# Decay tables of a gated-DeltaNet / S5 trunk: built from a float32 product on TensorE instead of from broadcast loads, and stored once per chunk from ScalarE's queue

## The chip, the cores and the metric

The kernel runs on one core of one Trainium2 chip. The metric is the device time of one execution in microseconds (us), the median of several runs. "PE" is TensorE's matmul stream, "PEld" its weight loads, "DVE" VectorE, "ACT" ScalarE, "POOL" GpSimd, "SP" SyncE, which here does nothing but issue DMAs. "PEclk" is the share of full TensorE clock that was granted.

## What is computed

One layer over a prompt of 4096 frames and over 32 frames of a running stream, with D_MODEL 1024. Half of the width goes through a gated delta rule with 4 heads of 128, the other half through an S5 state space. The delta rule is evaluated in chunks; this kernel takes chunks of 128 frames, so 32 of them for the prompt and one for the short stream, 33 in all. The part of the reference that the change touches is the decay between two frames of a chunk, which scales both the triangular system and the attention inside the chunk:

```python
    gc = jnp.cumsum(g, axis=-1)
    diff = gc[..., :, None] - gc[..., None, :]
    decay = jnp.where(incl, jnp.exp(jnp.where(incl, diff, 0.0)), 0.0)
    kb = k * beta[..., None]
    lower = jnp.where(strict, jnp.einsum('nbhid,nbhjd->nbhij', kb, k) * decay, 0.0) + eye
    attn = jnp.where(incl, jnp.einsum('nbhid,nbhjd->nbhij', q, k) * decay, 0.0)
```

## The kernel before

The program has three parts, recorded one after the other, and a tile scheduler orders each engine's instructions at build time from that recording and from priorities.

**Part A** normalises x, writes it to DRAM as two float16 halves (`h_d`), projects the S5 input and the gate logits, runs the S5 scan in four blocks of 1024 frames, and works out the two gate projections `z` (`zproj`, lines 505 to 526). One unit of `zproj` takes 128 frames: two transposing DMAs from `h_d` into `hz0` and `hz1` (line 519, issued by SP, two buffers each), 24 matmuls of 128x128x512 (line 492), a tanh on ACT (line 524), a multiply on DVE (line 525), and a store to `z_d` issued by POOL (line 526). There are 33 units for the gate of the delta rule and then, after the weights in `wz` have been replaced, 33 for the gate of S5 (`zs`). They have a low priority and fill gaps.

At the end of part A come the **tables**. `gates` has left the running decay sums `gc` in DRAM (`gc_d`, one row of 128 per head and chunk), half the beta values in `be_d`, and minus the sums by partition in `ngC` (in the buffer `gcC`). For each chunk, `tables` (line 985) loads the row of sums of its four heads onto all 128 partitions (line 990, a broadcast from DRAM into `tdm`), and the betas likewise (line 992, into `tbr`); POOL sets everything under the diagonal to -1e30 (line 993); ACT takes four exponentials with the negative sums as bias (line 995); POOL multiplies betas and decay (line 997); SP stores both tables to `dm_d` (lines 998 and 999). `tdm` and `tbr` have three buffers each.

**Part B** runs the chunks. Four chunk generators (`par` 0 to 3) interleave with a stream of dense work (q/k/v projections, S5 output). Its pools take over the memory of part A, so the first chunk's loads wait for the last unit of `zproj`. A chunk (line 1436 on) loads the chunk's decay sums' exponentials into `gr` by a broadcast (line 1480) and its two tables into `br` and `dm` (lines 1482 and 1483). POOL multiplies `kn` by `ed` (line 1519) and `qT` by `gr` (line 1522); DVE multiplies the key product by `br` (line 1532, giving the triangular system `at` for `inverse`) and the query product by `dm` (line 1543). Line 1456 is the helper that splits a float32 tile into two float16 halves, and line 48 the helper through which most matmuls go.

**Part C** is the output projection of what part B left over.

Of the kernel before, what the change touches and what calls it, by code (L numbers as in the profile page):

```python
# [6 lines left out]
F32 = mybir.dt.float32  # L7
# [4 lines left out]
ALU = mybir.AluOpType  # L12
# [5 lines left out]
H = 4  # L18
# [17 lines left out]
class Drive:  # L36
# [3 lines left out]
    def __init__(self, nc):  # L40
        self.nc, self.t, self.streams = nc, 0.0, []
# [38 lines left out]
class Trunk:  # L80
    def __init__(self, ctx, tc, io, T):
        self.ctx, self.tc, self.nc, self.io, self.T = ctx, tc, tc.nc, io, T
        self.NB = T // 512
        self.NC = T // 128
        nc = self.nc
        self.pe = Drive(nc)
        self.ugs = []
        self.ws, self.un, self.uz, self.marks = {}, {}, {}, []
        self.cst = ctx.enter_context(tc.tile_pool(name="cst", bufs=1))
        self.sm = ctx.enter_context(tc.tile_pool(name="sm", bufs=2))  # L90
        self.dram = ctx.enter_context(tc.tile_pool(name="dram", bufs=1, space=DRAM))
        c = self.cst
        self.ident = c.tile([128, 128], F32, name="ident")
        self.ones_pool = ExitStack()
        self.ones = self.pool(self.ones_pool, "a_one").tile([128, 128], F32, name="ones")
        nc.gpsimd.memset(self.ones, 1.0)
        nc.gpsimd.affine_select(out=self.ident, in_=self.ones, pattern=[[1, 128]], compare_op=ALU.is_equal,
                                fill=0.0, base=0, channel_multiplier=-1)
        self.mhalf = c.tile([128, 4], F32, name="mhalf")
        nc.gpsimd.memset(self.mhalf, -0.5)  # L100
        self.ident16 = c.tile([128, 128], F16, name="ident16")
        nc.vector.tensor_copy(self.ident16, self.ident)
        self.h_d = [self.dram.tile([2, 1024, 1024], F16, name=f"h_d{b}") for b in range(T // 1024)]
        self.hs_d = self.dram.tile([2, TS, 1024], F16, name="hs_d")
        self.us_d = self.dram.tile([512, 8, TS // 8], F32, name="us_d")
        self.ab_d = self.dram.tile([64, T // 1024, 128], F32, name="ab_d")
        self.abs_d = self.dram.tile([8, 128], F32, name="abs_d")
        self.gy_d = [self.dram.tile([4, 128, 1024], F32, name=f"gy_d{b}") for b in range(T // 1024)]
        self.gys_d = self.dram.tile([4, 128, TS], F32, name="gys_d")
        self.z_d = [self.dram.tile([1024, 512], F32, name=f"z_d{b}") for b in range(T // 1024)]  # L110
        self.zs_d = self.dram.tile([TS, 512], F32, name="zs_d")
        self.z5_d = [self.dram.tile([1024, 512], F32, name=f"z5_d{b}") for b in range(T // 1024)]
        self.z5s_d = self.dram.tile([TS, 512], F32, name="z5s_d")
        self.mx_d = [self.dram.tile([2, 256, 512], F16, name=f"mx_d{b}") for b in range(T // 256)]
        self.mxs_d = self.dram.tile([2, TS, 512], F16, name="mxs_d")
        self.m5_d = [self.dram.tile([2, 1024, 512], F16, name=f"m5_d{b}") for b in range(T // 1024)]
        self.m5s_d = self.dram.tile([2, TS, 512], F16, name="m5s_d")
        self.gc_d = {"p": self.dram.tile([H, self.NC, 128], F32, name="gc_d"), "s": self.dram.tile([H, 1, 128], F32, name="gcs_d")}
        self.be_d = {"p": self.dram.tile([H, self.NC, 128], F32, name="be_d"), "s": self.dram.tile([H, 1, 128], F32, name="bes_d")}
        self.eg_d = {"p": self.dram.tile([H, self.NC, 128], F32, name="eg_d"), "s": self.dram.tile([H, 1, 128], F32, name="egs_d")}  # L120
        self.dm_d = [self.dram.tile([2, 128, H, 128], F32, name=f"dm_d{c}") for c in range(self.NC + 1)]
        self.kp_d = self.dram.tile([16, 2, G, 240], F16, name="kp_d")


# [109 lines left out]
    def phase_a(self):  # L234
        nc, io = self.nc, self.io
# [53 lines left out]
        for blk in range(NK):  # L289
# [7 lines left out]
            if blk == NK - 3:  # L297
# [9 lines left out]
                f, ws = self.wfirst("zs", self.room_pr())  # L307
# [11 lines left out]
        bld = ExitStack()  # L319
# [13 lines left out]
        self.e_gy = cst.tile([128, 2], F32, name="e_gy")  # L333
        self.pow2(ma, self.e_gy[:, 0:1], self.e_gy[:, 1:2])
        self.right.close()
        tbl = self.pool(bld, "b_tbl")
        order = list(range(self.NC))
        order.insert(2 * SP, self.NC)
        with self.tc.high_priority(offset=-250):
            for ci in order:  # L340
                self.tables(tbl, ci)
        self.phase_b1()
        bld.close()
        left.close()
# [637 lines left out]
        self.ngC = self.gcC  # L982
        v.tensor_single_scalar(self.ngC, self.gcC, -1.0, op=ALU.mult)

    def tables(self, pool, ci):

        nc = self.nc
        key, cd = ("p", ci) if ci < self.NC else ("s", 0)
        dm = pool.tile([128, H, 128], F32, name="tdm", bufs=3)
        nc.sync.dma_start(dm, self.gc_d[key][:, cd].partition_broadcast(128))  # L990
        br = pool.tile([128, H, 128], F32, name="tbr", bufs=3)
        nc.sync.dma_start(br, self.be_d[key][:, cd].partition_broadcast(128))
        nc.gpsimd.affine_select(out=dm, in_=dm, pattern=[[0, H], [1, 128]], compare_op=ALU.is_ge, fill=-1e30, base=0, channel_multiplier=-1)  # L993
        for h in range(H):
            self.last_exp = nc.scalar.activation(dm[:, h], dm[:, h], AF.Exp, bias=self.ngC[:, h, ci:ci + 1])  # L995
            self.after(self.last_exp, self.last_gelu)
        nc.gpsimd.tensor_tensor(br, br, dm, op=ALU.mult)
        nc.sync.dma_start(self.dm_d[ci][0], dm)
        nc.sync.dma_start(self.dm_d[ci][1], br)

    def scales(self):

# [421 lines left out]
    def chunk(self, ci, c, b, key, par):  # L1424

        nc, ck, pc, pe = self.nc, self.ck, self.pc, self.pe
        pf = self.pf
        v, gp, act = nc.vector, nc.gpsimd, nc.scalar
# [5 lines left out]
        def t4(nm, dt=F32, n=128):  # L1434
            return ck.tile([128, H, n], dt, name=f"{nm}{par}")
# [4 lines left out]
        def col(t):  # L1440
            return t[:, :, ci:ci + 1].to_broadcast([128, H, 128])
# [4 lines left out]
        def tmp():  # L1446
            return ck.tile([128, H, 128], F32, name="tp", bufs=2)

        def halves(t):
            return t.rearrange("p h c -> p (h c)").bitcast(F16).rearrange("p (x h c) -> p x h c", x=2, h=H)  # L1450

        def pair(t, src, eng=gp):

            t, n = halves(t), src.shape[-1]
            act.copy(t[:, 0, :, :n], src)
            eng.tensor_tensor(t[:, 1, :, :n], src, t[:, 0, :, :n], op=ALU.subtract)
            return t
# [21 lines left out]
        cd = ci if key == "p" else 0  # L1479
        nc.sync.dma_start(gr, self.eg_d[key][:, cd].partition_broadcast(128))  # L1480
        br, dm = t4("br"), t4("dm")
        nc.sync.dma_start(br, self.dm_d[ci][1])
        nc.sync.dma_start(dm, self.dm_d[ci][0])

        yield lambda: not self.busy
        while self.busy:
# [31 lines left out]
        t = tmp()  # L1518
        gp.tensor_tensor(t, kn, col(self.ed), op=ALU.mult)
        kd = pair(kn, t)  # L1520
        t = tmp()
        gp.tensor_tensor(t[:, :, :m], qT[:, :, ts], gr[:, :, :m], op=ALU.mult)
        if m < 128:
# [18 lines left out]
        t = tmp()  # L1542
# [338 lines left out]
```

## Time and profile before

| | us |
|---|---|
| median of 3 runs (lowest, highest) | 2684.92 (2680.22, 2686.32) |
| the profiled execution | 2683.79 |
| its span | 2682.1 |
| PE busy | 2106.2 (79%) |
| DVE busy | 1588.1 (59%) |
| ACT busy | 1203.1 (45%) |
| POOL busy | 973.6 (36%) |
| SP's DMA queue, share of 16 DMA engines | 44.9% |

The busy shares are means over parts that differ: part A ends at some 1180 us of the span, part B at some 2300 us. The page's row of 40 slices shows PE at 3 to 4 tenths from slice 10 to slice 15, where it is at 7 to 9 tenths before and after; that stretch is where the tables are made.

### The profile page before, as it was taken

Reading aid. Unit: us, or ns where it says so; the run is one execution under the profiler, and the core shown is the slowest. Engines: PE = TensorE matmul, PEld = TensorE weight load, DVE = VectorE, ACT = ScalarE, POOL = GpSimd, SP = SyncE. Lnnn points to the kernel's source line nnn. Section 1 sums busy time; section 2 is a strip of 40 time slices with the busy share of each in tenths; the row PEclk is TensorE's granted clock in tenths of the full one; section 3 lists DMA queues with packets and bytes.
Section 4 is the critical chain, followed back from the end, with each engine's and each line's share of the span. In section 5 each row is a group of like instructions: output and inputs, shape, how many; then the busy total and the mean of one; then the engine's idle time right before and its main releaser. Section 6 shows DMA issues by size and latency. Waiting matters only on the chain.

```text
span 2682.1 us, 47343 instructions
## 1 busy us (share of the span) xinstructions
PE 2106.2 (79%) x17712; PEld 1481.7 (55%) x17712; DVE 1588.1 (59%) x3855; ACT 1203.1 (45%) x3400; POOL 973.6 (36%) x1080
## 2 busy tenths in 40 slices
PE   3887788768374445888988788788988986899998
PEld 3544666645142112546767677677777874454443
DVE  3796665777151000336978789877878897533222
ACT  5355455324352111225666566666656766321111
POOL 1354354434122122123554455445544554310000
PEclk9988899879687777989999999899989997899999
DMA  4489577366876778353223332222313235256552
GB/s 150 147 200 220 117 161 161 59 71 129 149 179 132 138 146 162 79 106 77 69 65 81 72 79 75 72 70 76 77 59 78 78 99 135 61 150 176 148 149 82
DMA packets 498847, 303.94 MB, mean 113 GB/s; under 512 B 346676, under 2 KB 447256, under 8 KB 498104
## 3 DMA queue, kind: packets, MB, share of 16 engines
q1 hardware_dynamic: 488392, 266.85, 44.9%
q0 software_dynamic: 10224, 34.06, 4.2%
q8 instruction: 138, 2.26, 0.4%
q14 instruction: 93, 0.76, 0.1%
HBM read 128.22 MB, written 94.88 MB: 83 GB/s over the span
## 4 chain that ended last, share of the span: by engine, by line
PE 29%; DVE 15%; DMA 9%; issue 5%; ACT 5%; POOL 3%; SPq 2%; POOLq 0%; DVEq 0%; ACTq 0%
PE pp L48 15%; PE po L48 7%; DVE acc L1332 3%; PE pz L492 3%; PE bk L48 3%; DMA hz<-h_d 3%; DMA m_d<-gh 3%; ACT jk L1495 1%; DMA tdm<-gc_d 1%; PE bk L52 1%; DVE kn L1596 1%; SPq L519 1%; DVE qT L1338 1%; DVE ubd L1653 1%; DMA tbr<-be_d 1%
## 5 line engine op out<-in xcount | busy, mean ns | idle before, releaser
L492 PE MATMUL pz<-wz,hz 128*128 128x512 f16 (+1 forms) x1464 | 390.3, 411 | 207.3 <-DMA hz<-h_d 178.5
L492 PEld LDWEIGHTS <-hz 128*128 128x128 f16 (+1 forms) x1464 | 148.1, 104 | 417.9 <-DMA hz<-h_d 211.7
L1332 DVE SCALAR_TENSOR_TENSOR acc<-pp,cwu,acc 128x256 f32<-128x256 f32 x540 | 256.1, 477 | 60.5 <-ACT acc L1330 54.9
L48 PEld LDWEIGHTS <-mx 128*128 128x128 f16 (+1 forms) x1584 | 154.3, 98 | 185.1 <-issue 3.5
L48 PE MATMUL pp<-h,wv 128*128 128x259 f16 (+1 forms) x1632 | 215.2, 274 | 25.5 <-DVE wei L360 19.6
L48 PE MATMUL pp<-h,wk 128*128 128x259 f16 (+1 forms) x1632 | 219.5, 289 | 6.1 <-ACT wk L207 5.3
L500 PE MATMUL pp<-wa,ht 128*128 128x260 f16 x1536 | 190.8, 279 | 20.5 <-ACT wa L207 11.8
L48 PE MATMUL pp<-h,wq 128*128 128x259 f16 (+1 forms) x1632 | 199.0, 274 | 7.7 <-DVE acc L1332 7.7
L525 DVE SCALAR_TENSOR_TENSOR zt<-zt,pz 128x512 f32<-128x512 f32 (+1 forms) x66 | 44.9, 681 | 262.3 <-ACT zt L524 262.1
L48 PE MATMUL po<-wo,mx 128*128 128x512 f16 (+1 forms) x912 | 197.2, 379 | 0.3 <-ACT th L1162 0.3
L48 PEld LDWEIGHTS <-wk 128*128 128x128 f16 x1632 | 162.0, 105 | 53.3 <-issue 13.0
L500 PEld LDWEIGHTS <-ht 128*128 128x128 f16 x1536 | 150.7, 100 | 49.3 <-issue 22.2
L48 PEld LDWEIGHTS <-wv 128*128 128x128 f16 x1632 | 149.2, 99 | 49.3 <-issue 23.6
L48 PEld LDWEIGHTS <-wq 128*128 128x128 f16 x1632 | 149.4, 99 | 28.9 <-issue 7.2
L48 PE MATMUL pp<-wo,mx 128*128 128x512 f16 x672 | 149.1, 382 | 0.0
L995 ACT ACTIVATE tdm<-tdm,gcC 128x128 f32<-128x128 f32 x132 | 42.3, 389 | 201.2 <-POOL tdm L993 191.2
L48 PE MATMUL pp<-wg,gh 128*128 128x512 f16 (+1 forms) x396 | 106.3, 405 | 31.1 <-ACT gh L207 29.4
L1495 ACT ACTIVATE jk<-bk 128x128 bf16<-128x128 f32 x396 | 109.7, 277 | 30.8 <-PE bk L48 11.6
L1330 ACT ACTIVATE acc<-pp,cwu 128x256 f32<-128x256 f32 x180 | 85.4, 474 | 68.3 <-PE pp L48 58.6
L129 POOL TENSOR_TENSOR rq_c<-ssc,mhalf 128x2 f32<-128x2 f32 (+1 forms) x17 | 11.7, 688 | 281.9 <-DVE ssc L1778 281.9
L48 PEld LDWEIGHTS <-a 128*128 128x128 f16 x1320 | 81.0, 101 | 47.5 <-issue 28.1
L48 PEld LDWEIGHTS <-knT 128*128 128x128 f16 x1188 | 85.3, 107 | 28.7 <-issue 19.9
(597 smaller groups left out, 4934.9 us busy)
## 6 DMA issues: line engine op xcount, KB each, us to landing
xn<-in_x SPq DMA_DIRECT2D x32, 512.0 KB, 4.3
h_d<-hl POOLq DMA_DIRECT2D x32, 512.0 KB, 5.2
z_d<-zt POOLq DMA_DIRECT2D x64, 256.0 KB, 4.1
xt<-in_x SPq DMA_DIRECT2D x18, 512.0 KB, 4.6
out_y<-xt SPq DMA_DIRECT2D x18, 512.0 KB, 3.3
dm_d<-tdm SPq DMA_DIRECT2D x33, 256.0 KB, 6.2
dm_d<-tbr SPq DMA_DIRECT2D x33, 256.0 KB, 6.9
br<-dm_d SPq DMA_DIRECT2D x33, 256.0 KB, 4.5
```

What stands on the lines that cost most here:

```text
L48: return self.nc.tensor.matmul(out, lhs, rhs, start=start, stop=stop)
L52: return self.nc.tensor.transpose(out, src, ident)
L492: self.nc.tensor.matmul(ps, a[x][:, c], w[:, y, c], start=c == 0 and x == y == 0, stop=c == K - 1 and x == 1)
L500: self.nc.tensor.matmul(pu[hf][:, :260], ht[x][:, c, :m], self.w_a[:, y, c, 260 * hf:260 * hf + 260], start=c == 0 and x == y == 0, stop=c ...
L519: nc.sync.dma_start_transpose(t, rows(self.h_d[blk][x] if blk >= 0 else self.hs_d[x]))
L525: nc.vector.scalar_tensor_tensor(zt, zt, 1.0, pz, op0=ALU.add, op1=ALU.mult)
L995: self.last_exp = nc.scalar.activation(dm[:, h], dm[:, h], AF.Exp, bias=self.ngC[:, h, ci:ci + 1])
L1330: nc.scalar.activation(acc, ps[:, 0:n], AF.Copy, scale=cw[:, e, 0:1])
L1332: v.scalar_tensor_tensor(acc, ps[:, j:j + n], cw[:, e, j:j + 1], acc, op0=ALU.mult, op1=ALU.add)
L1338: m1 = v.scalar_tensor_tensor(dst[:, h], th, 1.0, acc, op0=ALU.add, op1=ALU.mult)
L1495: act.activation(junk, src[:, h], AF.Square, accum_out=out[:, h:h + 1])
L1596: v.scalar_tensor_tensor(o[:, h], po[:m, h], ro[:m, h:h + 1], zc[:m, h], op0=ALU.mult, op1=ALU.mult)
```

## The change

The table's sums are no longer loaded onto all partitions. One load brings all rows of `gc_d` into the tile `gcr` (one row per head and chunk on a partition), and for each head a float32 matmul with one column of the identity, broadcast to 128 columns, copies that row onto all 128 partitions of a PSUM bank (`pt`, two buffers). DVE adds a constant tile `low` that is 0 on and above the diagonal and -1e30 under it, and writes `tdm` (three buffers); ACT takes the four exponentials as before and issues the store itself. The second table is not made any more: the chunk loads the betas by a broadcast and POOL multiplies them by the decay there.

```diff
-        self.dm_d = [self.dram.tile([2, 128, H, 128], F32, name=f"dm_d{c}") for c in range(self.NC + 1)]
+        self.dm_d = [self.dram.tile([128, H, 128], F32, name=f"dm_d{c}") for c in range(self.NC + 1)]
...
-        tbl = self.pool(bld, "b_tbl")
+        self.tbl = self.pool(bld, "b_tbl", 3)
+        self.pt = self.pool(bld, "b_pt", 2, psum=True)
+        self.low = self.tbl.tile([128, 128], F32, name="low", bufs=1)
+        nc.gpsimd.memset(self.low, 0.0)
+        nc.gpsimd.affine_select(out=self.low, in_=self.low, pattern=[[1, 128]], compare_op=ALU.is_ge, fill=-1e30, base=0, channel_multiplier=-1)
+        self.gcr = {key: self.tbl.tile([128, 128], F32, name="gc" + key, bufs=1)[:n] for key, n in (("p", H * self.NC), ("s", H))}
+        for key, t in self.gcr.items():
+            nc.sync.dma_start(t, self.gc_d[key].rearrange("h c t -> (h c) t"))
...
-        dm = pool.tile([128, H, 128], F32, name="tdm", bufs=3)
-        nc.sync.dma_start(dm, self.gc_d[key][:, cd].partition_broadcast(128))
-        br = pool.tile([128, H, 128], F32, name="tbr", bufs=3)
-        nc.sync.dma_start(br, self.be_d[key][:, cd].partition_broadcast(128))
-        nc.gpsimd.affine_select(out=dm, in_=dm, pattern=[[0, H], [1, 128]], compare_op=ALU.is_ge, fill=-1e30, base=0, channel_multiplier=-1)
+        gc, c, n = (self.gcr["p"], ci, self.NC) if ci < self.NC else (self.gcr["s"], 0, 1)
+        ps = self.pt.tile([128, H, 128], F32, name="pt")
+        k = H * n
+        for h in range(H):
+            p = h * n + c
+            nc.tensor.matmul(ps[:, h], self.ident[:k, p:p + 1].to_broadcast([k, 128]), gc, start=True, stop=True)
+        dm = self.tbl.tile([128, H, 128], F32, name="tdm")
+        nc.vector.tensor_tensor(dm, ps, self.low.unsqueeze(1).to_broadcast([128, H, 128]), op=ALU.add)
         for h in range(H):
             self.last_exp = nc.scalar.activation(dm[:, h], dm[:, h], AF.Exp, bias=self.ngC[:, h, ci:ci + 1])
             self.after(self.last_exp, self.last_gelu)
-        nc.gpsimd.tensor_tensor(br, br, dm, op=ALU.mult)
-        nc.sync.dma_start(self.dm_d[ci][0], dm)
-        nc.sync.dma_start(self.dm_d[ci][1], br)
+        nc.scalar.dma_start(self.dm_d[ci], dm)
...
         br, dm = t4("br"), t4("dm")
-        nc.sync.dma_start(br, self.dm_d[ci][1])
-        nc.sync.dma_start(dm, self.dm_d[ci][0])
+        nc.sync.dma_start(br, self.be_d[key][:, cd].partition_broadcast(128))
+        nc.sync.dma_start(dm, self.dm_d[ci])
...
         kd = pair(kn, t)
+        gp.tensor_tensor(br, br, dm, op=ALU.mult)
```

The scheduler orders the engines anew; lines after the first insertion move down by 8 (`zproj`'s transposes from 519 to 527). Three places show what moved.

SP's queue where the units of `zproj` for `zs` begin, before (`hz` are the transposes for `zproj`, `tdm`, `tbr` and `dm_d` the tables, `gyt` is S5 output's input):

```order
L998 DMA dm_d4_129<-tdm_8431 128x512
L999 DMA dm_d4_129<-tbr_8433 128x512
L519 DMA_TRANSPOSE hz0_5522<-h_d0_74 128x8x128
L519 DMA_TRANSPOSE hz1_5524<-h_d0_74 128x8x128
L990 DMA tdm_8445<-gc_d_119 128x4x128
L992 DMA tbr_8447<-be_d_121 128x4x128
L990 DMA tdm_8459<-gc_d_119 128x4x128
L992 DMA tbr_8461<-be_d_121 128x4x128
L1393 DMA gyt_9371<-gy_d0_82 128x4x128
L990 DMA tdm_8473<-gc_d_119 128x4x128
L992 DMA tbr_8475<-be_d_121 128x4x128
```

The same place of SP's queue now:

```order
L527 DMA_TRANSPOSE hz0_5489<-h_d0_74 128x8x128
L527 DMA_TRANSPOSE hz1_5491<-h_d0_74 128x8x128
L527 DMA_TRANSPOSE hz0_5522<-h_d0_74 128x8x128
L419 DMA hl_8813<-in_w_v 128x1024
L527 DMA_TRANSPOSE hz1_5524<-h_d0_74 128x8x128
L527 DMA_TRANSPOSE hz0_5555<-h_d0_74 128x8x128
L419 DMA xn_8810<-in_w_v 128x1024
L419 DMA xn_8811<-in_w_v 128x1024
L527 DMA_TRANSPOSE hz1_5557<-h_d0_74 128x8x128
```

Four DMAs per table stood between the transposes; none of them is left on SP there.

PE now, where the weights `wz` are replaced (`pt` is the new product, `pz` the product of `zproj`; the last `pz` of the old weights, `wz_189`, and the first of the new, `wz_5307`):

```order
L1001 MATMUL pt_8433<-gcp_8369,ident_63 128x128 x4
L1001 MATMUL pt_8445<-gcp_8369,ident_63 128x128 x4
...
L500 LDWEIGHTS hz1_5276
L500 MATMUL pz_5278<-wz_189,hz1_5276 32x512
L1001 MATMUL pt_8457<-gcp_8369,ident_63 128x128 x4
L1001 MATMUL pt_8469<-gcp_8369,ident_63 128x128 x4
L1001 MATMUL pt_8481<-gcp_8369,ident_63 128x128 x4
L500 LDWEIGHTS hz0_5357
L500 MATMUL pz_5361<-wz_5307,hz0_5357 128x512
```

Five tables stand within eight matmuls of `zproj` there, and two more within the next unit; from there on the tables are spread, one or two to a unit.

POOL inside one chunk now (`br` is line 1529's tile, the rest belongs to chunks that run beside it):

```order
L1635 TENSOR_TENSOR al0_14514<-br0_13625,ah0_14512 128x512
L1464 TENSOR_TENSOR tp_14635<-vb2_13071,tp_14635 128x512
L1464 TENSOR_TENSOR dm0_13626<-tp_14456,dm0_13626 128x512
L129 TENSOR_TENSOR rq_k_14587<-sk1_14575,mhalf_70 128x4
L1529 TENSOR_TENSOR br2_14896<-br2_14896,dm2_14897 128x512
```

The new multiply of chunk generator 2 has been put among the work of generators 0 and 1.

## Rows read from the trace of the kernel before

**Rows 1.** Busy time of each engine in three stretches of the span.
```profile
core 0: us, PE busy (x) PEld busy (x) DVE busy (x) ACT busy (x) POOL busy (x), PEclk, DMA share, GB/s
700.00:1060.00 360.00, 172.92 (x812) 85.84 (x811) 58.86 (x140) 100.43 (x260) 76.02 (x91) 0.73 0.78 154
1060.00:1180.00 120.00, 110.55 (x624) 60.76 (x622) 40.37 (x114) 24.70 (x44) 23.02 (x42) 0.97 0.39 94
1180.00:2300.00 1120.00, 940.99 (x10540) 795.22 (x10539) 903.64 (x2277) 698.43 (x2202) 560.07 (x544) 0.91 0.32 80
```
**Rows 2.** Waits of PE, 700 to 1060 us (total, times, longest).
```profile
PE pz L492 <- DMA hz<-h_d: 159.1, 22, 16.8
PE pp L48 <- DVE wei L360: 19.6, 1, 19.6
```
**Rows 3.** Waits of PE, 1060 to 1180 us.
```profile
PE pz L492 <- DMA hz<-h_d: 0.6, 1, 0.6
```
**Rows 4.** DMA issues, 700 to 1060 us (count, KB each, median us to landing).
```profile
dm_d<-tbr SPq DMA_DIRECT2D x33, 256.0 KB, 6.9
tdm<-gc_d SPq DMA_DIRECT2D x30, 256.0 KB, 9.4
hz<-h_d SPq DMA_TRANSPOSE x39, 10.2
```
**Rows 5.** DMA issues, 1060 to 1180 us.
```profile
q1 hardware_dynamic: 26752, 7.47, 29.8%
q0 software_dynamic: 1120, 3.67, 8.8%
z_d<-zt POOLq DMA_DIRECT2D x14, 256.0 KB, 3.3
hz<-h_d SPq DMA_TRANSPOSE x24, 3.6
```
**Rows 6.** SP's timeline (start, us, line).
```profile
926.02 5.77 SPq L519 DMA_TRANSPOSE hz<-h_d  x1
...
586.44 21.01 SPq L519 DMA_TRANSPOSE hz<-h_d  x8
```
**Rows 7.** PE groups, 700 to 1060 us, and PE's timeline elsewhere.
```profile
L492 PE MATMUL pz<-wz,hz 128*128 128x512 f16 x444 | 128.0, 444 | 159.1 <-DMA hz<-h_d 159.1
...
1110.09 3.83 PE L492 MATMUL pz<-wz,hz 128*128 128x512 f16 x17
608.06 0.66 PE L886 MATMUL pq<-x,wo 128*128 128x128 f32 x4
```
**Rows 8.** The group of the tables' exponentials on ACT, 700 to 1060 us.
```profile
L995 ACT ACTIVATE tdm<-tdm,gcC 128x128 f32<-128x128 f32 x132 | 42.3, 389 | 201.2 <-POOL tdm L993 191.2 <-DMA dm_d<-tbr 10.0
```
**Rows 9.** DVE and POOL groups of part B, 1180 to 2300 us.
```profile
L1543 DVE SCALAR_TENSOR_TENSOR tp<-bk,dm 128x512 f32<-128x512 f32 x33 | 22.5, 681 | 1.0 <-issue 1.0
L1653 DVE TENSOR_TENSOR ubd<-us,bd 128x512 f16<-128x512 f16 x96 | 56.8, 592 | 0.9
L1338 DVE SCALAR_TENSOR_TENSOR qT<-th,acc 128x256 f32<-128x256 f32 x56 | 31.9, 573 | 6.6 <-ACT th L1337 3.4 <-PE bk L52 3.1
L1522 POOL TENSOR_TENSOR tp<-qT,gr 128x512 f32<-128x512 f32 x32 | 42.2, 1320 | 0.3 <-DMA gr<-eg_d 0.3
```
**Rows 10.** Durations min/median/max of two DVE lines in part B.
```profile
L1653 DVE TENSOR_TENSOR ubd<-us,bd x93: 401/424/1458, 1223.9 to 2249.4; 128x512 f16<-128x512 f16 x93
L1338 DVE SCALAR_TENSOR_TENSOR qT<-th,acc x56: 400/424/1382, 1246.8 to 2183.8; 128x256 f32<-128x256 f32 x56
```
**Rows 11.** One chunk's timeline in part B: POOL, then DVE.
```profile
1521.83 1.05 POOL L1519 TENSOR_TENSOR tp<-kn,ed 128x512 f32<-128x512 f32 x1 [4.16 <-ACT kn L1502]
...
1539.48 0.68 DVE L1532 SCALAR_TENSOR_TENSOR br<-bk,br 128x512 f32<-128x512 f32 x1
```
**Rows 12.** DMA issues, 1200 to 2250 us.
```profile
br<-dm_d SPq DMA_DIRECT2D x29, 256.0 KB, 4.1
gr<-eg_d SPq DMA_DIRECT2D x27, 256.0 KB, 8.3
```

More of the change, by code (lines that the diff above doesn't have):

```diff
@@ L340, in phase_a @@
             for ci in order:
-                self.tables(tbl, ci)
+                self.table(ci)
         self.phase_b1()
@@ L983, in gates, with table @@
         v.tensor_single_scalar(self.ngC, self.gcC, -1.0, op=ALU.mult)
-    def tables(self, pool, ci):
+    def table(self, ci):
         nc = self.nc
-        key, cd = ("p", ci) if ci < self.NC else ("s", 0)
-        dm = pool.tile([128, H, 128], F32, name="tdm", bufs=3)
-        nc.sync.dma_start(dm, self.gc_d[key][:, cd].partition_broadcast(128))
-        br = pool.tile([128, H, 128], F32, name="tbr", bufs=3)
-        nc.sync.dma_start(br, self.be_d[key][:, cd].partition_broadcast(128))
-        nc.gpsimd.affine_select(out=dm, in_=dm, pattern=[[0, H], [1, 128]], compare_op=ALU.is_ge, fill=-1e30, base=0, channel_multiplier=-1)
+        gc, c, n = (self.gcr["p"], ci, self.NC) if ci < self.NC else (self.gcr["s"], 0, 1)
[6 more added lines that the diff above has]
+        nc.vector.tensor_tensor(dm, ps, self.low.unsqueeze(1).to_broadcast([128, H, 128]), op=ALU.add)
         for h in range(H):
```

## The prediction

> **What bounds the kernel now.** I read the busy time by stretches first. From 700 to 1060 us PE is busy 172.9 of 360 us at a granted clock of 0.73, and the 16 DMA engines at 0.78; before part B starts, from 1060 to 1180, PE is busy 110.6 of 120 us at 0.97 and the DMA engines at 0.39 [rows 1]. No engine is full in the first of these stretches, so something makes PE wait. The view of PE's waits names it: 159.1 of its 187 idle us end with a transposing load of `zproj` [rows 2]; in the next stretch, with the same units of `zproj` and no tables, 0.6 us do [rows 3]. So the tables do not wait on PE, they keep PE from being fed. The DMA issues say how: a transpose lands 10.2 us after its issue beside the tables, 3.6 us without them [rows 4, 5], and SP needs 5.77 us to issue one there, but 21.01 us for eight in an undisturbed place, 2.6 us each with the waits for buffers [rows 6]. SP's queue is in order, and the first order listing has four table DMAs in it between two units.
>
> How much DMA time the tables take can be worked out. Without tables the SP queue takes 29.8% of 120 us, 35.8 us, for 24 transposes and a few smaller transfers, so some 1.3 us of all 16 engines per transpose; a plain 256 KB store takes 8.8% of 120 over 14, 0.75 us [rows 5]. From 700 to 1060 us, 0.78 x 360 = 281 us are taken [rows 1]; 39 transposes make 51 [rows 4], and other loads and stores some 30. That leaves about 200 us for 33 tables, 6 us each: 1.5 for the two stores, and 2.3 for each broadcast load, three times a store of the same bytes.
>
> Part B is another matter: PE is busy 941 of 1120 us there, DVE 904, POOL 560 [rows 1]. It begins when the last unit of `zproj` has freed its memory, so time saved before 1180 us moves the whole rest forward.
>
> **The change, part by part**, on the 2683.8 us of the profiled execution (1.1 below the median of the runs).
>
> 1. *132 table DMAs leave SP, 33 stores come to ACT.* DMA time for tables falls from 200 to 33 x 0.75 = 25 us, and SP issues transposes only. I take the wait of 159.1 us down to 30. The lower bound is the 0.6 us of [rows 3], for 14 units; the upper one a third of the wait, 53, since landing times fall to a third. I take 30, a little over half way, because in a stretch of `zproj` alone two transposes (2 x 1.3 us of issue, 3.6 of landing [rows 5, 6]) take 6.2 us against 24 x 0.225 = 5.4 us of matmuls [rows 7], a loss of near 1 us for each of 18.5 units, and the stores still share the engines. **-129 us.** On issuing from ACT, the rules for kernel authors in the Trainium skill's "DMA: Bandwidth & Descriptors" say that spreading DMAs over issuing engines adds no bandwidth and saves issue time only. By that rule the moved store alone would be worth 33 issues of SP and nothing else; whoever credits the queue with the gain would be wrong by it, and no row here shows a DMA from ACT.
>
> 2. *PE's clock.* 444 matmuls of `zproj` take 128.0 us from 700 to 1060, 0.288 each; 17 in a row at full clock take 3.83 us, 0.225 each [rows 7]. What PE did before its clock fell was to stand idle half the time. PE's work of the stretch, 172.9 us at 0.73, is 126 us at full clock. With PE mostly busy I take 0.88, between 0.73 and the 0.97 of the next stretch [rows 1], so 143 us. **-30 us** (bounds 0 and -43).
>
> 3. *132 float32 matmuls of 128x128x128 on PE.* Four of them stand in 0.66 us at line 886 [rows 7]; 33 x 0.66 / 0.9 = **+24 us**. Bounds: 0 if they fall into waits, 48 at half clock.
>
> 4. *The table's new chain.* DVE's add from PSUM is like line 1543, 0.681 us [rows 9]; the four exponentials stay, 4 x 0.389 [rows 8]; ACT's issue is taken as 0.4, as SP needs for plain DMAs; the store lands in 3.3 to 6.9 us [rows 4, 5]. A table thus holds its `tdm` buffer for 6 to 9.5 us, and three buffers let one through every 2 to 3.2 us, where a unit of `zproj` takes 5.4. DVE and ACT are busy 59 and 100 of 360 us [rows 1], so their work is covered; POOL's 33 selects and 33 multiplies go. But PE is in order: where the listing has seven tables within two units, PE waits for `pt`, which waits for `tdm`, which waits for a store, and the units behind it wait too. Most of that falls where PE waits for new weights anyway. I take **+25 us**; bounds 0 and 33 x 3.2 = 105 us, if no table is covered.
>
> 5. *Part B.* Each chunk gains a POOL multiply as in line 1522, 1.32 us [rows 9], 44 us in all on an engine with 560 idle us; the multiply has from 1521.8 to 1539.5, 18 us, in the chunk looked at [rows 11]. DVE loses time to POOL: line 1653 has median 424 and mean 592 ns, line 1338 424 and 573 [rows 9, 10], so 96 x 0.168 + 56 x 0.149 = 24 us in these two beside 560 us of POOL; 44 us more POOL costs 2 to 3. The betas come by a broadcast that lands in 8.3 us like `gr`, not 4.1 [rows 12]; the loads are issued a chunk ahead, so it shows at the first chunk only, some 4 us. **+10 us** with a little for DMA traffic; bounds 0 and 88 (two times 44).
>
> The sum is -129 - 30 + 24 + 25 + 10 = -100: **2584 us**. Kept are the 19.6 us for v's weights [rows 2] and the rest of the idle time; late next are those weights, and then PE itself.
>
> **The rivals.** (The measurement tells about 0.2%, 5 us, from no change.)
>
> A. *Everything falls into place.* The waits go to 0, the clock is 0.97, the new matmuls cost 23 us, the chain and part B nothing: -159 - 43 + 23 = -179, 2505 us. For it: the next stretch runs like that [rows 1, 3]. Against it: that stretch has q/k/v matmuls between the units, which hide the loads; most units before 1060 have none.
>
> B. *PE waits for tables instead of transposes.* Step 4 at its upper bound, 105 instead of 25: 2664 us. For it: the tables are spread over PE's in-order stream and have just two PSUM banks. Against it: 3.2 us per table beats 5.4 per unit.
>
> C. *Part B pays back more: slower.* The multiply stands in POOL's queue ahead of other chunks' work, and the triangular system waits for it; if all 1.32 us of it reach the path of each chunk, 44 us, and DVE is held for as long again, 88. With the gain of rival B's stage, 129 + 30 - 24 - 105 = 30 us, that is 2742 us; it decides from the point where the cadence of 1120 / 33 = 34 us per chunk grows by more than the first stage's gain over 33: 3.3 us for mine, 0.9 for B's. Against it: POOL is idle half of part B and line 1532 comes 18 us after line 1519 [rows 1, 11]. The Trainium skill's "SBUF — State Buffer", section "Who interferes with whom", has a DVE instruction with two SBUF inputs fully block against a POOL instruction that reads SBUF, for the whole instruction. By that rule each new multiply can hold DVE for its full 1.3 us; the longest cases of lines 1653 and 1338, 1458 and 1382 against 424 ns [rows 10], agree, and their means say that it is rare.
>
> D. *The change does not do what it says.* The transposes stay late, through SP's own 2-buffer waits or the stores from ACT; then only clock and the new work count, and it ends within 10 us of before. The 3.6 us of [rows 5] speak against it.
>
> **How the numbers follow.** My sum 0.52, A 0.15, B 0.18, C 0.10, D 0.05. The sum's own range is 2545 to 2625. The whole range, 2505 to 2675, takes in nearly all of that, half or more of A, and B up to some 90 us of chain, near 0.8; C and the rest are outside. Faster is the sum, A, B and a little of D, 0.86; same 0.04; slower 0.10.
>
> **What would show it.** Right: PE's wait for `hz` under 60 us from 700 us on, transposes landing in 4 to 5 us, a last unit of `zproj` about 110 us earlier, granted clock near 0.9; ACT's stores landing in about 4 us; part B within 15 us of its 1120 us; line 1532 not waiting for POOL. Wrong: PE's `pt` matmuls waiting for DVE by tens of us (B), DVE's at-multiply waiting for POOL and part B over 1150 us (C), or `hz` waits above 100 us with the DMA engines half idle (D).

## The result, and the profile after

The changed kernel takes 2548.35 us (median of four runs, 2546.6 to 2552.8), the kernel before 2684.44 beside it: ratio 0.9498, interval 0.948 to 0.9515. It is faster by 136 us, where 100 were forecast; 2548 lies in the range of 2505 to 2675, and in the likeliest case's own, 2545 to 2625. The time is right, and two terms behind it are not: the stage gave nearly twice what I had summed (204 us, not 110), and part B took some two thirds of the surplus back.

The boundary between the two is the first load of a chunk, `gr`, which SP issues when the stage is over. Before, that was at 1180.4 us. After:

```profile
L1488 SPq DMA_DIRECT2D gr<-eg_d x32: 359/360/974, 976.0 to 2126.3; - x32
```

So the stage ends 204.4 us earlier, and from there to the end it takes 2548.0 - 976.0 = 1572.0 us where it took 2682.1 - 1180.4 = 1501.7: **-204 and +70**.

The busy time of the engines by stretches, as in [rows 1]: the stage, the first chunk's loads, and 1120 us of part B.

```profile
core 0: us, PE busy (x) PEld busy (x) DVE busy (x) ACT busy (x) POOL busy (x), PEclk, DMA share, GB/s
700.00:976.00 276.00, 271.92 (x1652) 167.26 (x1652) 119.34 (x288) 120.58 (x286) 34.92 (x67) 1.00 0.61 146
976.00:1016.00 40.00, 20.62 (x347) 16.13 (x348) 19.77 (x31) 12.05 (x40) 21.12 (x25) 0.62 0.75 151
1060.00:2180.00 1120.00, 905.61 (x9903) 760.10 (x9900) 873.88 (x2195) 669.12 (x2105) 573.75 (x542) 0.89 0.32 74
```

In the stage PE is now idle for 4.1 of 276 us and is granted full clock, 2.4 GHz. Before, the row of 40 slices showed PE at 3, 7, 4, 4, 4 and 5 tenths in slices 10 to 15, not at 3 to 4 throughout. Up to 700 us the two kernels' PE is busy alike, 514.3 and 512.9 us. In part B it is a little less busy than before, at 0.89 instead of 0.91.

The stage's PE waits from 690 to 976 us are all here (total, times, longest), then its two main groups of PE and three of its DMA issues:

```profile
PE pt L1001 <- DVE mm L138: 18.1, 1, 18.1
PE pz L500 <- DMA hz<-h_d: 3.2, 3, 1.5
PE pt L1001 <- DVE tdm L1003: 0.8, 1, 0.8
```

```profile
L500 PE MATMUL pz<-wz,hz 128*128 128x512 f16 (+1 forms) x798 | 217.7, 381 | 3.3 <-DMA hz<-h_d 3.2
L1001 PE MATMUL pt<-gcp,ident 128*128 128x128 f32 x224 | 35.8, 287 | 18.9 <-DVE mm L138 18.1 <-DVE tdm L1003 0.8
```

```profile
z_d<-zt POOLq DMA_DIRECT2D x33, 256.0 KB, 3.6
dm_d<-tdm ACTq DMA_DIRECT2D x30, 256.0 KB, 4.0
hz<-h_d SPq DMA_TRANSPOSE x64, 4.3
```

The wait for transposes is gone (159.1 us in [rows 2]), they land in 4.3 us instead of 10.2 [rows 4], and the new product waits 0.8 us for a table's tile. The 18.1 us end before 700 us, on the maximum over the partitions ahead of the tables; near the same place the kernel before waited for the new weights `wz` (480 to 1180 us):

```profile
PE pz L492 <- DVE wz L208: 22.6, 1, 22.6
```

Part B is another picture. First the new multiply's group on POOL from 1180 to 2300 us, then SP's wait before the load of `dm` (1060 to 2166 us), then three of PE's waits from 976 us to the end:

```profile
L1529 POOL TENSOR_TENSOR br<-br,dm 128x512 f32<-128x512 f32 x26 | 33.0, 1269 | 110.8 <-DMA dm<-dm_d 106.8 <-ACT kn L1510 3.0 <-PE bk L48 1.0
```

```profile
SPq L1491 <- PE bk L48: 128.8, 26, 13.8
```

```profile
PE bk L48 <- POOL sp L1464: 29.5, 9, 9.6
PE bk L48 <- DVE p L1671: 20.5, 12, 3.5
PE bk L48 <- POOL tp L1464: 11.6, 9, 4.3
```

POOL stands 106.8 us before the multiply, waiting for `dm`. Before, from 1180 us to the end, PE's three waits took 0.7, 10.8 and 1.8 us; that for POOL's `sp` (the low half of the state) is as good as new. One chunk shows how they hang together: SP, POOL and PE from 1391 us on.

```profile
1391.77 0.82 SPq L1490 DMA_DIRECT2D br<-be_d  x1
1392.68 0.45 SPq L1491 DMA_DIRECT2D dm<-dm_d  x1
```

```profile
1391.12 1.15 POOL L1428 TENSOR_TENSOR gh<-gt,gh 128x512 f16<-128x512 f32 x1
1403.14 1.26 POOL L1529 TENSOR_TENSOR br<-br,dm 128x512 f32<-128x512 f32 x1 [10.87 <-DMA dm<-dm_d]
1404.36 1.15 POOL L1464 TENSOR_TENSOR sp<-S_p,sp 128x512 f16<-128x512 f32 x1
```

```profile
1405.57 0.69 PE L48 MATMUL bk<-sp,knT 128*128 128x128 f16 x5 [9.60 <-POOL sp L1464]
```

`dm` is issued at 1392.68, behind `br`, and the multiply starts at 1403.14. `sp` belongs to another chunk and was free to run (ACT had written its other half by 1392.2 us), but it stands behind the multiply, and PE waits 9.60 us for it. The DMA issues of part B, 1180 to 2250 us, complete the view: `br` lands in 8.8 us, `dm` behind it in 5.0, and `m_d`, a store of S5's output, in 7.2, where it was 4.1, 2.7 and 3.1 before ([rows 12] shows the first).

```profile
gr<-eg_d SPq DMA_DIRECT2D x26, 256.0 KB, 8.4
m_d<-gh SPq DMA_DIRECT2D x26, 256.0 KB, 7.2
br<-be_d SPq DMA_DIRECT2D x25, 256.0 KB, 8.8
dm<-dm_d SPq DMA_DIRECT2D x25, 256.0 KB, 5.0
```

### The profile page after: what moved, and what is told of

The parts are those of the page before. It is cut to its first block, busy times and chain, and to the rows that moved or that the text cites. A ratio compares the mean times of both kernels' runs of the same rounds, so it can differ in the third digit from the quotient of the medians.

```text
span 2548.0 us, 47554 instructions
## 1 busy us (share of the span) xinstructions
PE 2109.8 (83%) x17976; PEld 1513.1 (59%) x17976; DVE 1621.6 (64%) x3888; ACT 1202.6 (47%) x3400; POOL 952.1 (37%) x1049
## 3 DMA queue, kind: packets, MB, share of 16 engines
q1 hardware_dynamic: 457248, 232.31, 40.7%
## 4 chain that ended last, share of the span: by engine, by line
PE 39%; DVE 22%; DMA 13%; issue 10%; ACT 7%; POOL 6%; SPq 2%; DVEq 0%; POOLq 0%; ACTq 0%
PE pp L48 16%; PE pz L500 8%; PE po L48 7%; PE bk L48 4%; DMA dm<-dm_d 4%; DMA m_d<-gh 3%; DVE acc L1340 3%; DVE vv L869 2%; DMA hz<-h_d 1%; DMA gy_d<-vv 1%; PE pt L1001 1%; DVE vv L860 1%; DMA h_d<-hl 1%; PE bk L52 1%; PE pp L508 1%
## 5 line engine op out<-in xcount | busy, mean ns | idle before, releaser
L500 PE MATMUL pz<-wz,hz 128*128 128x512 f16 (+1 forms) x1464 | 383.9, 390 | 25.8 <-DMA hz<-h_d 20.3
L48 PE MATMUL pp<-h,wk 128*128 128x259 f16 (+1 forms) x1632 | 224.9, 284 | 0.0
L48 PE MATMUL pp<-h,wq 128*128 128x259 f16 (+1 forms) x1632 | 208.9, 272 | 0.1
L48 PE MATMUL pp<-wg,gh 128*128 128x512 f16 (+1 forms) x396 | 112.1, 421 | 36.8 <-ACT gh L207 35.5
L534 POOL DMA_DIRECT2D z_d<-zt x64 | 36.8, 575 | 212.7 <-DVE zt L533 201.8
L1784 DVE SCALAR_TENSOR_TENSOR xt<-po,uo,xt 128x512 f32<-128x512 f32 (+1 forms) x38 | 28.5, 749 | 118.7 <-PE po L48 118.7
```

The costliest lines, as they stand in the source:

```text
L48: return self.nc.tensor.matmul(out, lhs, rhs, start=start, stop=stop)
L500: self.nc.tensor.matmul(ps, a[x][:, c], w[:, y, c], start=c == 0 and x == y == 0, stop=c == K - 1 and x == 1)
L534: nc.gpsimd.dma_start(rows(dst[0][blk]) if blk >= 0 else dst[1], zt)
L1784: v.scalar_tensor_tensor(xt[:m, sl], ps, self.uo[:m], xt[:m, sl], op0=ALU.mult, op1=ALU.add)
```

## The experiments

Two questions: what in the 132 DMAs had held the stage, and which part of the new chunk code costs 70 us. In the table, the first load is that of `gr`, the stretch runs from there to the end of the span, both of the profiled run; the ratio is to the kernel before, whose medians beside these runs were 2671 to 2677 us.

| kernel | first load | stretch | median us | ratio, interval |
|---|---|---|---|---|
| before | 1180.4 | 1501.7 | 2684.44 | 1 |
| changed | 976.0 | 1572.0 | 2548.35 | 0.9498, 0.948 to 0.9515 |
| store on SP | 977.4 | 1570.9 | 2545.74 | 0.9516, 0.9494 to 0.9538 |
| unused loads on SP | 1112.6 | 1572.1 | 2686.44 | 1.0044, 1.0027 to 1.0061 |
| unused loads, by chunk | 1010.8 | 1563.3 | 2575.86 | 0.963, 0.9584 to 0.9677 |
| product with gr | 980.1 | 1592.5 | 2568.21 | 0.9604, 0.9582 to 0.9626 |
| no product | 975.1 | 1535.4 | 2515.24 | 0.9408, 0.9384 to 0.9433 |
| br from table, product | 976.9 | 1516.5 | 2495.81 | 0.9313, 0.9287 to 0.9339 |
| br from table, no product | 978.4 | 1495.6 | 2476.94 | 0.9248, 0.9223 to 0.9272 |
| product late | 976.6 | 1562.4 | 2546.86 | 0.9509, 0.9486 to 0.9531 |
| both tables by product | 1015.4 | 1506.1 | 2524.84 | 0.9428, 0.9411 to 0.9446 |
| be by chunk | 986.1 | 1507.3 | 2500.48 | 0.9355, 0.9328 to 0.9383 |
| be and eg by chunk | 983.1 | 1457.6 | 2440.3 | 0.9122, 0.9089 to 0.9154 |
| before, rows by chunk | 1041.0 | 1448.9 | 2491.77 | 0.9309, 0.9282 to 0.9337 |

The stretch is that of one execution, which lies up to some 6 us beside the median of its kernel, and the scheduler orders every kernel anew, so a few us of a stretch mean nothing. The four kernels "product with gr", "no product" and "br from table" leave a factor out or put another in its place, so they compute another matrix than the reference; only their times are used.

### The stage: queue or loads

```
-        nc.scalar.dma_start(self.dm_d[ci], dm)
+        nc.sync.dma_start(self.dm_d[ci], dm)
```

> The changed kernel with one edit: the 33 table stores are issued on SP's queue instead of ACT's. Theory Q (the stage was held by SP's queue: a store waits there for the four exponentials of its table, and the transposes that feed TensorE stand behind it): the hz waits of PE from 690 to 976 us go from 3 us to over 60, the first chunk load goes from 976 to between 1050 and 1130 us, and the time is 2620 to 2700 us. Theory L (the 66 broadcast loads, by their traffic and their issue, held the stage; which queue stores a table is all one): the first chunk load stays within 15 us of 976 and the time is 2540 to 2565 us. A middle (the stores are ready early now, since the tables need no loads, so a store on SP waits a microsecond or two): 33 x 1 to 2 us, 2580 to 2615 us.

Theory L holds; nothing changes: 977.4 us, and a ratio whose interval overlaps. SP does wait for the exponentials before a store, but briefly (total, times, longest from 600 to 976 us):

```profile
SPq L1007 <- ACT tdm L1005: 9.3, 10, 1.3
```

ACT's queue is worth nothing measurable here. That agrees with the rules for kernel authors in the Trainium skill's "DMA: Bandwidth & Descriptors", by which spreading DMAs over issuing engines saves issue time and adds no bandwidth.

```
+        for nm, src in (("xg", self.gc_d), ("xb", self.be_d)):
+            x = self.tbl.tile([128, H, 128], F32, name=nm, bufs=2)
+            nc.sync.dma_start(x, src[key][:, cd].partition_broadcast(128))
```

> The changed kernel with two more broadcast loads per table on SP's queue, the same 66 loads that the kernel before had, into tiles that nothing reads (two buffers each); the tables come from the product as in the changed kernel, so these loads add nothing to what is computed. Theory L (the loads held the stage): the first chunk load comes 100 us or more later than 976 us, transposes of hz land in 8 to 10 us again, and the time is 2640 to 2690 us. Theory Q (waits of stores in SP's queue): the loads wait for nothing but the load before them in the same buffer, hz waits stay under 30 us, time 2555 to 2580 us.

Theory L holds. The loads alone, read by nobody, move the first chunk load by 136.6 us and take the whole gain away. PE's wait for transposes from 690 to 1112 us and the loads' landing:

```profile
PE pz L500 <- DMA hz<-h_d: 81.6, 14, 24.5
```

```profile
xg<-gc_d SPq DMA_DIRECT2D x32, 256.0 KB, 9.1
xb<-be_d SPq DMA_DIRECT2D x32, 256.0 KB, 10.9
```

The other 68 us of the stage (1112.6 to 1180.4) are what the loads alone don't explain: the second table, the stores that wait in SP's queue for POOL, POOL's work. It is rather more than 68, since this kernel also has the new product's some 36 us of PE, which the kernel before has not. No run takes these apart.

### Part B: product or load

```
-        gp.tensor_tensor(br, br, dm, op=ALU.mult)
+        gp.tensor_tensor(br, br, gr, op=ALU.mult)
```

> The changed kernel with one operand replaced: POOL's new multiply in a chunk takes br times gr in place of br times dm. The product is then not the decay table that the step needs, so the state that the chunks hand on is another one; the number, shape and engine of all instructions are unchanged, and gr is a tile that POOL's next instruction needs anyhow. Theory W (part B's 70 us more come from POOL waiting in order for the late load of dm): the 112 us of POOL waits for dm go, and the stretch from the first chunk load to the end falls from 1572 to 1500 to 1530 us, time 2475 to 2510 us. Theory K (the 29 multiplies' own work on POOL, and what they take of VectorE's time): nothing changes, 2535 to 2560 us.

Both theories missed, since the edit did not do what I meant. `gr` comes later than `dm`, because its tile also holds the chunk's output until that is stored, and POOL waited longer than with `dm`, 107.8 us (1000 to 2300 us):

```profile
POOL br L1529 <- DMA gr<-eg_d: 177.0, 26, 15.3
```

It is a dose all the same: 70 us more of POOL's wait and 20 us more of time.

```
-        gp.tensor_tensor(br, br, dm, op=ALU.mult)
```

> The changed kernel without POOL's multiply in a chunk: the masked decays are left out of the factor br, so what the inverse works on is not the reference's matrix; all other instructions stand. Theory W: as with the operand replaced, 2475 to 2510 us, and within 10 us of that run. Theory K: the 33 multiplies of 1.26 us (42 us) and their effect on VectorE go, 2490 to 2515 us here but 2535 to 2560 us with the operand replaced. If neither run gains more than 15 us, the cause lies in the broadcast load of br (8.8 us to landing against 4.1) or in the order that the instructions were put in.

The stretch falls by 37 us to 1535, about half of the 70, so neither the wait for `dm` nor the multiply explains it all; the time, 2515.24, lies 0.2 us over K's range, and K's claim that only the multiply's own work counts fails. What remains of the chunk's change is the load of `br`. The next two runs complete a square: product or none, broadcast load or contiguous one.

```
-        nc.sync.dma_start(br, self.be_d[key][:, cd].partition_broadcast(128))
+        nc.sync.dma_start(br, self.dm_d[ci])
```

> The changed kernel without POOL's multiply and with br loaded from the stored table (256 KB in the layout of the tile, as the kernel before loads it) in place of the broadcast from be_d; br then holds the decays without the factor that the broadcast brings, so the inverse works on another matrix. The stretch from the first chunk load to the end was 1502 us before, 1572 with the change, 1535 without the multiply. Theory F (the broadcast load of br, 8.6 us to landing where the contiguous one took 4.5, is the other half): 1495 to 1510 us, time 2475 to 2495 us. Theory O (the rest comes from the order that the instructions were put in, or from where the stage left the work): 1525 to 1545 us, time 2505 to 2525 us.

> The changed kernel with POOL's multiply kept and br loaded from the stored table, contiguous, in place of the broadcast from be_d; the factor be is left out of the product (it becomes the square of the decays). If the two parts of the loss add (about 35 us each for the multiply and the broadcast load): 1530 to 1545 us from the first chunk load to the end, time 2505 to 2525 us. If the multiply's wait for dm is what counts and the broadcast load delays dm behind it in the queue: 1510 to 1525 us and POOL's wait for dm falls from 108 us to under 60 us. If the load's form does not count: 1565 to 1580 us, 2540 to 2560 us.

The square, in us of the stretch:

| | broadcast load of br | contiguous load of br |
|---|---|---|
| product | 1572.0 | 1516.5 |
| no product | 1535.4 | 1495.6 |

The load costs 40 us without the product and 56 with it, the product 21 with a contiguous load and 37 with the broadcast. Theory F holds: 1495.6 is the kernel before, within 6 us. With the product the time is that of the second case, in which the broadcast load delays `dm` behind it; POOL's wait for `dm` (960 to 2160 us) is shorter, though not under 60 us:

```profile
POOL br L1529 <- DMA dm<-dm_d: 68.0, 22, 8.2
```

How the load costs 40 us where there is no product can be read from the two kernels of the lower row. In some chunks the store `m_d` stands just behind `br` on SP's queue. Three such stores, whose landing the trace has in both kernels, took 4.9, 4.8 and 2.2 us with the contiguous load and 10.4, 8.3 and 6.5 with the broadcast one. The tile `gh` that they store comes free later, ACT waits for it, and PE for ACT. From the first chunk load to the end, the contiguous load first:

```profile
ACT gh L207 <- DMA m_d<-gh: 37.0, 12, 7.3
PE pp L48 <- ACT gh L207: 15.4, 7, 3.4
```

```profile
ACT gh L207 <- DMA m_d<-gh: 72.1, 15, 9.4
PE pp L48 <- ACT gh L207: 40.6, 9, 9.5
```

PE's idle time there is 183.4 and 221.4 us; this one wait of PE has 25 of the 38 us between them.

```
-        gp.tensor_tensor(br, br, dm, op=ALU.mult)
 ...
+        gp.tensor_tensor(br, br, dm, op=ALU.mult)
         at = br
```

> The changed kernel with POOL's multiply written later in a chunk: behind the product of qT and gr and its pair, directly ahead of the instruction that uses it; nothing else is changed and the result is the same. Theory W (POOL's queue stands behind the multiply that waits for dm): the wait goes to what is then ahead of it or is over by then; POOL's wait for dm falls from 108 us to under 50 us and the stretch from the first chunk load to the end from 1572 to 1540 to 1555 us, time 2505 to 2530 us. Theory K (the multiply's work and the br load): 1565 to 1580 us, 2535 to 2560 us; should the late multiply hold up VectorE's use of it, 2560 to 2580 us.

The median, 2546.86, lies in K's range and not in W's. Writing it later gains 10 us of the stretch and nothing in the median (the profiled execution is 6 us under it). The wait for `dm` is as long as it was; the multiply still stands ahead of other chunks' work, and PE still waits 24.1 us for `sp`.

```profile
POOL br L1539 <- DMA dm<-dm_d: 108.2, 26, 11.5
```

### Ways out

```
+            nc.tensor.matmul(pb[:, h], self.ident[:k, p:p + 1].to_broadcast([k, 128]), be, start=True, stop=True)
 ...
+        br = self.tbl.tile([128, H, 128], F32, name="tbr")
+        nc.vector.tensor_tensor(br, pb, dm, op=ALU.mult)
+        nc.scalar.dma_start(self.dm_d[ci][0], dm)
+        nc.scalar.dma_start(self.dm_d[ci][1], br)
 ...
-        nc.sync.dma_start(br, self.be_d[key][:, cd].partition_broadcast(128))
-        nc.sync.dma_start(dm, self.dm_d[ci])
+        nc.sync.dma_start(br, self.dm_d[ci][1])
+        nc.sync.dma_start(dm, self.dm_d[ci][0])
 ...
-        gp.tensor_tensor(br, br, dm, op=ALU.mult)
```

> Candidate: both tables made in the stage without broadcast loads. The rows of be are spread over the partitions by 132 more float32 matmuls into the same two PSUM buffers, VectorE multiplies them with the decays (33 more multiplies), and both tables are stored on ACT's queue; the chunk is as in the kernel before. From the rows: TensorE, which is 92 to 100 per cent busy in the stage, gets 132 x 0.275 us = 36 us more; VectorE's 33 x 0.7 us = 23 us lie beside it; the chunks' stretch goes back from 1572 to about 1502 us. First chunk load at 976 + 25 to 45 us = 1000 to 1020 us, time 2500 to 2525 us. If the two PSUM buffers, each now held until VectorE has multiplied, make TensorE wait: 33 x 1 to 2 us more, 2535 to 2590 us.

As worked out: the stage is 39 us longer, because PE is full there, and part B is the kernel before's. The second product's group, 690 to 1016 us:

```profile
L1007 PE MATMUL pt<-bep,ident 128*128 128x128 f32 x256 | 36.2, 279 | 0.0
```

But why is a broadcast load of 256 KB slower than a contiguous one? `be_d` lies by head, so each partition's 2 KB come as four pieces of 512 bytes. Laid by chunk they are one piece:

```
-self.dram.tile([H, self.NC, 128], F32, name="be_d")
+self.dram.tile([self.NC, H, 128], F32, name="be_d")
 ...
-        nc.sync.dma_start(br, self.be_d[key][:, cd].partition_broadcast(128))
+        nc.sync.dma_start(br.rearrange("p h t -> p (h t)"), self.be_d[key][cd].rearrange("h t -> (h t)").partition_broadcast(128))
```

> The changed kernel with one layout changed: be_d lies in DRAM by chunk (chunk, head, position) instead of by head, so the broadcast load of br reads one piece of 2 KB for each partition where it read four of 512 bytes; the store that fills be_d is split in four, far ahead of the stage. The result is the same. Theory P (the broadcast load of br is slow because it is in 512-byte pieces): br lands in 3 to 4.5 us instead of 8.6, dm behind it in 3 us instead of 4.8, and the stretch from the first chunk load to the end falls from 1572 to about the 1516 us that the contiguous load of a stored table gave (1510 to 1530); time 2490 to 2512 us. Theory B (128 readers of the same bytes are slow, whatever the pieces): br still lands after 7 us or more and the stretch stays over 1555 us, time 2530 to 2555 us.

> As the run with be_d by chunk, and eg_d by chunk too, so that the load of gr (8.4 us to landing, in the kernel before as well) is in pieces of 2 KB. Theory P: gr lands in 3 to 4.5 us too; if a broadcast load of gr costs the chunk what one of br did (40 to 55 us over the stretch), it is 1460 to 1485 us and the time 2440 to 2465 us; if gr is needed late enough to be hidden, 1505 to 1520 us and 2485 to 2500 us. Theory B: no change against the changed kernel, 2530 to 2555 us.

Theory P holds in both: the medians lie in its ranges, each stretch 2 to 3 us below. Landing times with both laid by chunk, 1180 to 2050 us, against the four rows of the changed kernel above; and the two kernels' lines of SP's queue, packets first, the changed kernel's and then this one's:

```profile
gr<-eg_d SPq DMA_DIRECT2D x26, 256.0 KB, 3.0
br<-be_d SPq DMA_DIRECT2D x25, 256.0 KB, 3.5
dm<-dm_d SPq DMA_DIRECT2D x25, 256.0 KB, 2.6
m_d<-gh SPq DMA_DIRECT2D x23, 256.0 KB, 3.0
```

```profile
q1 hardware_dynamic: 457248, 232.31, 40.7%
```

```profile
q1 hardware_dynamic: 432672, 232.31, 40.5%
```

24576 packets fewer for the same bytes are 64 loads (32 of `br`, 32 of `gr`) with 128 pieces instead of 512. `be` by chunk is worth 65 us of the stretch, `eg` another 50, though no line of the change touches `gr`. The kernel before already had one such load: the short stream is a single chunk, so its four rows lie together, and the trace has 128 packets of 2 KB for it. It landed in 3.1 us, where the others took 8.3 [rows 12] (1200 to 2250 us):

```profile
gr<-egs_d SPq DMA_DIRECT2D x1, 256.0 KB, 3.1
```

The kernel with both laid by chunk is the best of the study: 2440.3 us, 4% under the changed one by the two ratios (0.9122 / 0.9498 = 0.960).

> The kernel before, with only the layout of gc_d, be_d and eg_d changed to lie by chunk, so that its 66 broadcast loads in the stage and 33 loads of gr in part B are in pieces of 2 KB; all else as it was. It tells whether the loads held the stage by their pieces or by being there. Theory P: the table loads land in 4 to 5 us instead of 9.7, hz transposes in 5 us instead of 8 to 10, the first chunk load comes 60 to 150 us before 1180, and gr's part gives 0 to 40 us in part B: 2490 to 2610 us. Theory Q' (the 66 loads and 66 stores in SP's in-order queue with their waits held it): the first chunk load stays within 30 us of 1180 and the time is 2625 to 2680 us.

Theory P holds, near the lower end of its range. The kernel before with the layout alone gains 139 us in the stage and 53 in part B, and so more in all than the change did (0.9309 against 0.9498), with all 132 table DMAs on SP. In the stage alone the change gave more, 204 us; the layout wins by part B, where it gains 53 (expected were 0 to 40) and the change loses 70. From 690 to 1041 us:

```profile
PE pz L492 <- DMA hz<-h_d: 53.2, 22, 10.8
```

```profile
tdm<-gc_d SPq DMA_DIRECT2D x32, 256.0 KB, 5.3
tbr<-be_d SPq DMA_DIRECT2D x32, 256.0 KB, 5.6
```

> As the run with 66 unused broadcast loads on SP's queue, which took back the whole gain (first chunk load at 1112.6 us against 976.0, ratio to the kernel before 1.004), but the unused loads read copies of the rows that lie by chunk, in pieces of 2 KB; the same 66 entries in SP's queue and the same bytes, in a quarter of the pieces. Chunks load as in the changed kernel. Theory P (the 512-byte pieces held the stage): the first chunk load comes at 985 to 1030 us and the time is 2545 to 2600 us. Theory Q' (the 66 entries in SP's in-order queue, each waiting for the load before it in its buffer, held it): 1080 to 1115 us and 2645 to 2690 us. Between these, the share of each by where it falls.

Theory P holds here too, with a part of Q'. The same 66 entries in SP's queue cost 35 us in pieces of 2 KB and 137 in pieces of 512 bytes (1010.8 and 1112.6 against 976.0). So some 100 us of the unused loads' cost go with their 512-byte pieces, and 35 with their being there at all. From 690 to 1010 us:

```profile
PE pz L501 <- DMA hz<-h_d: 24.6, 9, 6.2
```

## Why the prediction was right, and where it was wrong

The time came right because the stage beat its sum by 94 us and part B missed its own by 60. That two misses of opposite sign partly cancel is luck.

1. *The table DMAs leave SP* (-129). Mechanism right, size off. PE's idle time from 700 us to the first chunk load was 187.1 + 9.4 = 196.5 us before [rows 1] and is 4.1 after: **-192**. The wait went to 3.2 us where I left 30; I held against rival A that units without other matmuls between them would wait for their transposes. That was not put to the test: in the new order the units have the product or q/k/v matmuls between them (from 840 to 890 us, 171 of `zproj` beside 120 of q and k). The waits for late weights, which I kept, went too. I put the cause on SP's queue and DMA time. The run with unused loads confirms the loads, the one with copies by chunk that of the 137 us they cost some 100 go with their 512-byte pieces, the one with the store on SP that the queue of the stores does not count. My own rows had the clue, a broadcast load at three times the price of a store of the same bytes; I used the price and did not ask for its reason.

2. *The clock* (-30). Right, and more: 1.00, not 0.88. PE's work up to the first chunk load was 172.92 x 0.73 + 110.55 x 0.97 = 233.5 us at full clock where it took 283.5: **-50**, beyond my bound, which had only the first of these stretches.

3. *The product* (+24). Too low: 35.8 us in the group above, with 224 records for 28 tables: a float32 matmul is two records (17976 of PE in all against 17712, 264 more for 132 matmuls). All 33 tables take 41.5. The four in 0.66 us of [rows 7] were two matmuls, so one costs near 0.3 us, not 0.165. Within the bounds of 0 and 48.

4. *The table's chain* (+25). It cost 0.8 us after 700 us; the wait of 18.1 us before that stands near where the kernel before waited 22.6 us for weights, as the prediction had it. Three buffers and two PSUM banks were enough, and rival B with them is out.

These give -192 - 50 + 36 + 1 = -205, against 204.4 measured: the stage is rival A's, more so.

5. *Part B* (+10). The step that failed, at **+70**. From the first chunk load to the end, before and after (columns as in [rows 1]):

```profile
1180.40:2682.10 1501.70, 1308.03 (x12425) 968.71 (x12425) 1031.15 (x2525) 760.98 (x2339) 594.58 (x580) 0.93 0.36 93
976.00:2548.00 1572.00, 1324.96 (x12434) 978.30 (x12434) 1043.70 (x2525) 762.10 (x2339) 636.52 (x613) 0.91 0.36 89
```

PE's idle time grew by 53 us (193.7 to 247.0), its busy time by 17, at a granted clock of 0.91 instead of 0.93. The sentence that failed is "the loads are issued a chunk ahead, so it shows at the first chunk only". They are not: SP waits 128.8 us for PE before `dm`, whose tile holds the attention of its generator's last chunk until the output is made, and `br` lands late enough to delay it further. SP's wait itself is not new; the kernel before had it too (1180 to 2300 us):

```profile
SPq L1483 <- PE bk L48: 120.8, 27, 10.6
```

Before, `dm` was needed only at line 1543, behind the first product, and that line waited for no load [rows 9]; the new multiply needs it earlier. I looked at when the multiply's result was used (18 us later, [rows 11]) and not at when its operands arrive, though the trace of before showed it.

Rival C had the place right, POOL's multiply in the queue ahead of other chunks' work, and the cadence: 70 / 33 = 2.1 us per chunk, under the 3.3 from which it would have decided for my stage, which came out larger still. But the triangular system did not wait for POOL: line 1541 (1532 before) waited 4.9 us in all, for PE. What waited was other chunks' work. Its second half, VectorE held as long again, did not come: DVE's busy time rose by 12.6 us in the two rows above, POOL's by 41.9. Lines 1653 and 1338 had means of 592 and 573 ns in [rows 9], and the same instructions now have (1180 to 2300 us)

```profile
L1662 DVE TENSOR_TENSOR ubd<-us,bd 128x512 f16<-128x512 f16 x82 | 46.6, 568 | 0.8
L1346 DVE SCALAR_TENSOR_TENSOR qT<-th,acc 128x256 f32<-128x256 f32 x48 | 30.1, 630 | 2.7 <-ACT th L1345 2.6
```

one lower, one higher. And of the 76 us between the corners of the square the larger share, 40 to 56, goes to a cause that I had priced at 4: the broadcast load of `br`. Rival D is out.

What stays open: why pieces of 512 bytes delay a load. The queue's packets took 40.7% of 2548.0 us and 40.5% of 2440.7, a difference of 49 us over 64 loads or 0.8 us each of all 16 engines, while a load lands 5 us earlier; the engines' work does not explain that. The packet records of the traces show when the packets start. In 22 loads of `gr` of the kernel before, beside which no other 512-byte packets run, the 512 packets start over 6.8 us (median), 75 in a us, and take 47 ns each on the mean. In three loads of `gr` in the kernel before with rows by chunk, the 128 packets of 2 KB start over 1.7 us, 75 in a us as well. So in these loads the time follows the number of packets. What sets their rate is not shown, nor whether it is the size of the pieces or that the four of a partition lie 16 KB apart: laying by chunk changes both. No view here tells the engines apart. Nor was it tried to give the attention a tile of its own, so that `dm` could be loaded earlier.

## What to carry to other kernels

When loads of the same bytes land at different speeds in a profile, look at how many pieces each is made of before moving work to another engine: a layout of three small tensors in DRAM was worth 185 us in all, making the tables elsewhere 136, and the change with two of the three laid by chunk 236. When a change makes an operand needed earlier on an in-order engine, read when that operand's tile comes free and its load lands, not only when the result is used; what waits is everything behind it. The same holds for a slow load: where there was no product, most of its price came through a store that stood behind it. And a sum that comes out right in total should still be checked by stretches.

## What the runs showed of the hardware

In part B a broadcast load of 256 KB landed in 8.4 to 8.8 us in pieces of 512 bytes and in 3.0 to 3.5 us in pieces of 2 KB; packets of `gr` started at some 75 a us in both forms. In the changed kernel the plain store `m_d` landed in 7.2 to 9.8 us in the five known cases that stand up to 6 us behind a load in 512-byte pieces on the same queue, in 2.1 to 4.2 us in the four others. The specifications in the Trainium skill's "DMA: Bandwidth & Descriptors" give 512 bytes as the smallest transfer for full rate; here loads in pieces of just that size took two to three times as long to land as in pieces of 2 KB, and the measurement decides. A float32 matmul of 128 columns shows as two records and takes PE some 0.28 to 0.32 us.
